# Three moved pieces at the start of a four-layer kernel: decay rates, condition columns and rotation tables

## The chip, the cores and the metric

The kernel runs on one core of a Trainium2 chip. The metric is device time in microseconds (us) of one execution, the median of three runs. The core has five engines with a queue of instructions each: PE (matmul), DVE (vector), ACT (activation), POOL (GpSimd) and SP, which here only issues DMAs. Each queue is executed in its order; an instruction whose semaphores have not come holds up everything behind it on its engine.

## The reference

The input `x` is 256 rows of 1024. Two layers of a first model are applied to it (`first_block`): an even layer, whose one projection gives query, key, value, gates and the input `u` of a diagonal state-space scan, and an odd layer (indexed attention). Then two layers of a second model (`second_block`), which is conditioned on a vector `c` and has a second stream of rows, the context.

```python
# even layer of the first block (cut)
q, k, v, gate_a, u, gate_b = split_cols(hn @ w_in, EVEN_SPLITS)
q, k = rms_norm(q, q_g), rms_norm(k, k_g)
att = swa_sink_attention(q, k, v, sinks, rel_bias) * silu(gate_a)
ssm = s5_mixer(u, log_dt, a_re, a_im, ...) * silu(gate_b)   # x_t = a * x_(t-1) + b u_t
# second block (cut)
mod   = silu(c) @ ada_w[i] + ada_b[i]                       # six rows of shifts, scales, gates
mod_c = silu(c_ctx) @ ada_w[i] + ada_b[i]
# its second layer is a chunked scan (SSD) with the decay rates
A = -exp(A_log)
```

## The kernel before

The program is written in Tile: the Python text gives every instruction with its engine and a priority (the order in which it is written), and a scheduler sets the order in which each engine's queue holds them. A change of the text near the start therefore also changes the order of work far behind it.

**Weights.** A weight tile is 128x1024 words (512 KB). SP issues its DMA into one of three `raw` buffers (L167), ACT makes a rounded high part `h` (L178), DVE the remainder `l` (L179), and PE multiplies both with the high and low part of the normalised rows (`nhx`, `nlx`), for each 128 columns or rows: high times high and low, then remainder times high. There are two buffers each of `h` and `l`.

**The start.** The rows are normalised and transposed in eight pieces; ACT writes `nhx` (L329), DVE `nlx` (L330). Then PE makes, in the text's order, `u` from weight tiles 1 to 4 (`pu`), the query from tiles 5 to 8 and key and value from 9 and 10 (`pdx`), and the gates from 11 to 18 (`pg`). Beside this DVE prepares the state-space parameters (`sv`, `fr`, `bb`, `bd`, L466 to L539), whose pieces PE transposes (`pbt`, `pct`).

**Query and key norm** (`head_norm`, `rstd`): ACT squares, DVE sums (`ss`, L405), POOL makes the mean (L285) and the power -1/2 (L286), DVE multiplies (`qn`, L407), PE transposes (`pqt` for the query, `pkt` for the key). This is done once for each half of the rows: query half 0, query half 1, key half 0, key half 1.

**The rotation tables.** The scan is turned into a real one by cosines and sines for 256 positions; POOL makes them from the small tables `tr` (L642 to L647, six instructions of 128x512 for two of the sixteen states' groups) in the tile `tabs`. The first two sets, twelve instructions, are for `q == 0`.

**The decay rates** (end of `late_params`, L372 to L379): a DMA of 64 words `A_log`, a power on POOL (L373), three small DVE steps (L374 to L376), one PE product and a copy to `A_row`. They lie in the tile `rp`, which also holds the other late parameters. `A_row` is read only in the last layer (`step_sizes`).

**The condition columns** (`cond_columns`): two small DMAs (`crows`), a tanh on ACT, a DVE step, one PE transpose (`pcc`, L864) and one DVE copy to `cT` (L866). All products `pada` of the condition with `ada_w` (L894, weights in `aw` and `araw`, 512 KB each) need `cT`. They are called from `ctx_start`, a hook of the even layer, and PE uses them to fill its time.

Of the kernel before, what the change touches and what calls it, by code (L numbers as in the profile page):

```python
# [8 lines left out]
F32 = mybir.dt.float32  # L9
# [3 lines left out]
ALU = mybir.AluOpType  # L13
# [75 lines left out]
def build(tc, A):  # L89
# [5 lines left out]
    def D(name):  # L95
        return A[name]

    def dram(a, off, ap):
        return bass.AP(tensor=a.tensor, offset=a.offset + off, ap=ap)
# [26 lines left out]
    marks = {}  # L126
# [6 lines left out]
    def after(mark):  # L133
        return tc.issue_after(marks[mark]) if mark is not None else ExitStack()
# [146 lines left out]
    def rstd(ss, n, cnt, key):  # L281
        t = wk.tile([128, 16], F32, tag="rs0" + key[:1])
        r = wk.tile([128, 16], F32, tag="rs1" + key[:1])
        with tc.high_priority(offset=WPRI):
            G.tensor_scalar(t[:, :cnt], ss, 1.0 / n, 1e-6, op0=ALU.mult, op1=ALU.add)  # L285
            G.tensor_tensor(r[:, :cnt], t[:, :cnt], nhalf[:, :cnt], op=ALU.pow)  # L286
        return r[:, :cnt]

    sums = {}
# [62 lines left out]

    def late_params():
        rp = cx.tile([128, 512], F32, tag="ntc", name="rp")
        pa_r, pb_r, a_diag = rp[:, 0:128], rp[0:96, 128:256], rp[0:64, 256:320]
        a_log, a_pos = rp[0:64, 320:321], rp[0:64, 321:323]
        V.memset(pa_r, 0.0)
        for r0, name, n in ((16, "norm_mix_g_2", 16), (32, "norm_ffn_g_2", 16),
                            (48, "ev_glu_b", 8), (56, "ev_ssm_d", 4), (60, "ssm_norm_g_2", 16),
                            (80, "ssm_conv_b_2", 32)):  # L360
            rows(pa_r, r0, name, n)
        for r, name, n in ((76, "ev_q_norm_g", 64), (77, "ev_k_norm_g", 64), (78, "od_q_norm_g", 128),
                           (79, "od_k_norm_g", 128)):
            SY.dma_start(pa_r[r:r + 1, :], dram(D(name), 0, [[0, 1], [0, 128 // n], [1, n]]))
        rows(pb_r, 0, "ssm_conv_w_2", 96)
        pp = psx.tile([128, 512], F32, tag="m")
        T.transpose(pp[:, 0:128], pa_r, ident)
        T.transpose(pp[:, 128:224], pb_r, ident[:96, :96])
        V.tensor_copy(par[:, 16:224], pp[:, 16:224])
        for lo, hi in ((60, 76), (80, 112), (128, 224)):  # L370
            V.tensor_scalar(par[:, lo:hi], pp[:, lo:hi], 0.5, None, op0=ALU.mult)
        SY.dma_start(a_log, dram(D("ssm_A_log_2"), 0, [[1, 64], [1, 1]]))  # L372
        G.tensor_tensor(a_pos[:, 0:1], ebase[0:64, 0:1], a_log, op=ALU.pow)  # L373
        V.tensor_scalar(a_log, a_log, -e_del, 1.0, op0=ALU.mult, op1=ALU.add)  # L374
        V.scalar_tensor_tensor(a_pos[:, 1:2], a_pos[:, 0:1], -1.0, a_log, op0=ALU.mult, op1=ALU.mult)
        V.tensor_scalar(a_diag, ident[0:64, 0:64], a_pos[:, 1:2], None, op0=ALU.mult)  # L376
        pp = psx.tile([128, 512], F32, tag="m", name="pp")
        mm(pp[:, 0:64], m_le[0:64, 127:128].to_broadcast([64, 128]), a_diag, True, True)
        V.tensor_copy(A_row, pp[:, 0:64])  # L379
# [41 lines left out]
    def even_layer(hook):  # L421
        with ExitStack() as st:
# [2 lines left out]
            NW = 2304  # L425
            actk = norm_T(xt, g_norm[:, 0:8], None, "x", psx)
            wx.on_pool = LP[0]

            uT = p.tile([128, 4, 256], F32, name="uT")
            QT = p.tile([128, 4, 256], F32, name="QT")  # L430
# [199 lines left out]
            for q in range(4):  # L630
                py = psx.tile([128, 512], F32, tag="m", name="py")
                for jj in range(2):
                    ct, sn = (tabs[:, jj, z_] for z_ in range(2))
                    x1 = xp1
                    i4 = slice(4 * q + 2 * jj, 4 * q + 2 * jj + 2)

                    def hi(z):
                        return z[:, i4, 16:32][:, :, :, None].to_broadcast([128, 2, 16, 16])

                    def lo(z):  # L640
                        return z[:, i4, 0:16][:, :, None, :].to_broadcast([128, 2, 16, 16])
                    G.tensor_tensor(ct, hi(cos_), lo(cos_), op=ALU.mult)  # L642
                    G.tensor_tensor(x1, hi(sin_), lo(sin_), op=ALU.mult)
                    G.tensor_tensor(ct, ct, x1, op=ALU.subtract)
                    G.tensor_tensor(sn, hi(sin_), lo(cos_), op=ALU.mult)
                    G.tensor_tensor(x1, hi(cos_), lo(sin_), op=ALU.mult)
                    G.tensor_tensor(sn, sn, x1, op=ALU.add)  # L647
                    for j in range(2 * jj, 2 * jj + 2):
                        i = 4 * q + j
                        pv = psx.tile([128, 2, 256], F32, tag="m", name="pv")  # L650
                        for ri in range(2):
                            mm(pv[:, ri], BT[32 * j:32 * j + 32, ri, q], uT[32 * j:32 * j + 32, q], True, True)
                        cb = ct[:, j % 2].rearrange("p a b -> p (a b)")[:, None, :].to_broadcast([128, 2, 256])
                        sb = sn[:, j % 2].rearrange("p a b -> p (a b)")[:, None, :].to_broadcast([128, 2, 256])
                        m1 = sl.tile([128, 2, 256], F32, tag="m1", bufs=2)
                        m2 = sl.tile([128, 2, 256], F32, tag="m2", bufs=2)
                        V.tensor_tensor(m1, pv, cb, op=ALU.mult)
                        V.tensor_tensor(m2, pv, sb, op=ALU.mult)
                        G.tensor_tensor(m1[:, 0], m1[:, 0], m2[:, 1], op=ALU.subtract)
                        G.tensor_tensor(m1[:, 1], m1[:, 1], m2[:, 0], op=ALU.add)  # L660
                        mg = mag[:, i:i + 1].to_broadcast([128, 256])
                        for ri in range(2):
                            V.tensor_tensor_scan(m1[:, ri], mg, m1[:, ri], 0.0, op0=ALU.mult, op1=ALU.add)
                        V.tensor_tensor(m2, m1, sb, op=ALU.mult)
                        for ri in range(2):
                            V.scalar_tensor_tensor(m1[:, ri], m1[:, ri], (1.0, -1.0)[ri], cb[:, ri],
                                                   op0=ALU.mult, op1=ALU.mult)
                        o = py[32 * j:32 * j + 32, 0:256]
                        cs = slice(32 * j, 32 * j + 32)
                        mm(o, CT[:, 0, q, cs], m1[:, 0], True, False)  # L670
                        mm(o, CT[:, 1, q, cs], m1[:, 1], False, False)
                        mm(o, CT[:, 0, q, cs], m2[:, 1], False, False)
                        mm(o, CT[:, 1, q, cs], m2[:, 0], False, True)
                y = uT[:, q]
                y2 = xw.tile([128, 256], F32, tag="ntx", name="y2")
                V.scalar_tensor_tensor(y, y, ssm_d[:, q:q + 1], py[:, 0:256], op0=ALU.mult, op1=ALU.add)
                S.activation(y2, y, AF.Square)
                V.tensor_scalar(y2, y2, 0.044715, 1.0, op0=ALU.mult, op1=ALU.add)
                V.tensor_tensor(y2, y2, y, op=ALU.mult)
                S.activation(y2, y2, AF.Tanh, scale=math.sqrt(2 / math.pi))  # L680
                V.scalar_tensor_tensor(y, y2, 1.0, y, op0=ALU.add, op1=ALU.mult)
                if q in (1, 2):
                    attention(2 - q)
# [172 lines left out]
    def cond_columns():  # L856
        cr2 = cx.tile([16, 256], F32, tag="adaev", name="crows")
        cr, th = cr2[:, 0:128], cr2[:, 128:256]
        rows(cr, 0, "c_2", 8)
        SY.dma_start(cr[8:16], dram(D("c_ctx_2"), 0, [[128, 8], [1, 128]]))  # L860
        S.activation(th, cr, AF.Tanh, scale=0.5)
        V.scalar_tensor_tensor(th, th, 1.0, cr, op0=ALU.add, op1=ALU.mult)
        pt = psc.tile([128, 512], F32, tag="m", name="pcc")
        T.transpose(pt[:, 0:16], th, ident[:16, :16])  # L864
        V.memset(cT, 0.0)
        V.tensor_scalar(cT[:, :, 0:2].rearrange("p k v -> p v k"), pt[:, 0:16].rearrange("p (v k) -> p v k", v=2),  # L866
                        0.5, None, op0=ALU.mult)
# [270 lines left out]
    cst_ = {}  # L1138

    def ctx_start():  # L1140
        cond_columns()
        ada_rows(0)
        for grp in range(2):
            ada_pe(0, grp)
        ada_finish(0, 0, 2)
# [360 lines left out]
    hooks = {0: [c_start], 1: [c_qkv, c_attend]}  # L1506
    sc_b = even_layer(lambda i: [f() for f in hooks[i]])
    odd_layer(sc_b)
    c_ffn()
    x_attention()  # L1510
    tc.cur_priority += 2000000
# [31 lines left out]
```

## Time and profile before

| | before |
|---|---|
| median of 3 runs | 1568.19 us (1567.0 to 1572.32) |
| profiled execution: its own time, its span | 1569.01 us, 1567.2 us |
| PE, DVE, ACT, POOL busy | 1479.1, 1110.6, 771.3, 304.2 us |
| mean granted PE clock | 0.975 |

A row of a group or a timeline gives times in us from the span's start; "idle before" is the time in which that engine did nothing just ahead, and the arrow names what ended it. The granted clock is a share of full speed.

### The profile page before, as it was taken

The page shows a single profiled execution, that of the slowest core. Times are in us where ns is not written, and L with a number is a line of the kernel's source. Part 1 is how long each engine was busy: PE and PEld are TensorE (multiplying, and loading weights), DVE is VectorE, ACT ScalarE, POOL GpSimd, SP SyncE. Part 2 cuts the span into 40 slices and gives each one's busy share as a digit, 9 for nine tenths or more (in the row PEclk, how much of TensorE's full clock was granted, in tenths as well). Part 3 has the DMA queues.
Part 4 walks back from the last instruction along what each step waited for, and adds up shares of the span by engine and source line. Part 5 has one row for each costly group of instructions (what it writes and reads, how often), then busy time and mean ns, then how long its engine had stood idle before and what let it go on. Part 6 is the DMA issues. An engine that isn't in the chain of part 4 may idle for free. (4 is left out here: it accounts for less than half of the span.)

```text
span 1567.2 us, 26910 instructions
## 1 busy us (share of the span) xinstructions
PE 1479.1 (94%) x10532; PEld 1263.1 (81%) x10532; DVE 1110.6 (71%) x1825; ACT 771.3 (49%) x1386; POOL 304.2 (19%) x247
## 2 busy tenths in 40 slices
PE   6799998999999999999989999889899999799998
PEld 5574555786898888687779999888789998699997
DVE  6779996667766778666556665478988876665665
ACT  4433446654545455576444444445455544454444
POOL 2415660000100100000000000238966400200000
PEclk9899999999999999999999999898999999999999
DMA  8784565566665767633666465454534433455664
GB/s 252 237 224 143 185 172 164 142 190 211 192 187 169 219 204 201 224 109 101 199 209 190 161 186 181 126 135 123 128 106 129 109 97 121 156 164 187 194 188 135
DMA packets 306174, 264.56 MB, mean 169 GB/s; under 512 B 27441, under 2 KB 260703, under 8 KB 306048
## 3 DMA queue, kind: packets, MB, share of 16 engines
q1 hardware_dynamic: 306048, 262.85, 56.2%
q8 instruction: 83, 1.36, 0.4%
q14 instruction: 43, 0.35, 0.1%
HBM read 261.47 MB, written 1.34 MB: 168 GB/s over the span
## 5 line engine op out<-in xcount | busy, mean ns | idle before, releaser
L179 DVE TENSOR_TENSOR l<-raw,h 128x1024 fp32r<-128x1024 f32 (+2 forms) x366 | 453.4, 1241 | 268.0 <-ACT h L178 237.6
L178 ACT ACTIVATE h<-raw 128x1024 fp32r<-128x1024 f32 (+2 forms) x374 | 389.0, 1042 | 411.2 <-PE pdx L129 103.9
L129 PE MATMUL pffnx<-nhx,h 128*128 128x256 f32 x704 | 170.4, 282 | 0.0
L129 PE MATMUL pffnx<-nlx,h 128*128 128x256 f32 x704 | 170.1, 282 | 0.2 <-DVE nlx L349 0.2
L129 PEld LDWEIGHTS pffnx<-nhx,h 128*128 128x128 f32 x704 | 134.3, 191 | 1.6 <-issue 1.6
L129 PEld LDWEIGHTS pffnx<-nlx,h 128*128 128x128 f32 x704 | 133.9, 190 | 1.5 <-issue 0.8
L307 POOL TENSOR_TENSOR sums<-sums,nhalf 128x1 f32<-128x1 f32 x20 | 13.0, 652 | 536.3 <-DVE sums L303 523.4
L129 PE MATMUL pffnx<-nhx,l 128*128 128x256 f32 x704 | 96.8, 280 | 0.0
L129 PE MATMUL pffnc<-nhc,h 128*128 128x256 f32 x352 | 88.9, 287 | 0.4 <-ACT nhc L348 0.4
L129 PEld LDWEIGHTS pffnx<-nhx,l 128*128 128x128 f32 x704 | 88.4, 189 | 0.4 <-issue 0.4
L129 PE MATMUL pffnc<-nlc,h 128*128 128x256 f32 x352 | 87.9, 285 | 0.1
L179 POOL TENSOR_TENSOR l<-raw,h 128x1024 fp32r<-128x1024 f32 (+1 forms) x8 | 18.5, 2312 | 353.8 <-PE pdx L129 200.5
L129 PE MATMUL pdx<-h,nhx 128*128 128x256 f32 (+1 forms) x256 | 84.8, 347 | 1.4 <-DVE cv L1284 1.3
L129 PE MATMUL pdx<-h,nlx 128*128 128x256 f32 (+1 forms) x256 | 83.0, 341 | 0.0
L894 PE MATMUL pada<-araw,cT 128*32 128x256 f32 x704 | 72.7, 401 | 10.7 <-DMA araw<-ada_w 9.8
L129 PE MATMUL pcvx<-nhx,h 128*128 128x256 f32 x256 | 73.8, 298 | 3.8 <-DVE cv L1284 3.8
L129 PE MATMUL pdx<-h,fh 128*128 128x256 f32 (+1 forms) x264 | 77.2, 318 | 0.0
L129 PE MATMUL pdx<-h,fl 128*128 128x256 f32 (+1 forms) x264 | 77.1, 317 | 0.0
L129 PE MATMUL pcvx<-nlx,h 128*128 128x256 f32 x256 | 71.8, 290 | 0.0
L129 PEld LDWEIGHTS pffnc<-nhc,h 128*128 128x128 f32 x352 | 66.5, 189 | 2.9 <-ACT nhc L348 1.0
L129 PEld LDWEIGHTS pffnc<-nlc,h 128*128 128x128 f32 x352 | 66.6, 189 | 2.1 <-DVE nlc L349 0.5
L129 PE MATMUL pdx<-l,nhx 128*128 128x256 f32 (+1 forms) x256 | 58.5, 344 | 1.4 <-DVE l L179 1.3
(620 smaller groups left out, 3875.9 us busy)
## 6 DMA issues: line engine op xcount, KB each, us to landing
araw<-ada_w SPq DMA_DIRECT2D x88, 512.0 KB
raw<-ffn_w_gate SPq DMA_DIRECT2D x66, 512.0 KB
raw<-ffn_w_up SPq DMA_DIRECT2D x66, 512.0 KB
raw<-ffn_w_down SPq DMA_DIRECT2D x54, 512.0 KB
raw<-ssm_w_in SPq DMA_DIRECT2D x48, 512.0 KB
raw<-od_w_in SPq DMA_DIRECT2D x25, 512.0 KB
raw<-attn_w_qkv SPq DMA_DIRECT2D x24, 512.0 KB
raw<-attn_w_o SPq DMA_DIRECT2D x32, 256.0 KB
```

The source lines that it names most:

```text
L129: i = T.matmul(out, l, r, start=start, stop=stop)
L178: S.activation(h[:, :n], raw[:, :n], AF.Copy)
L179: (G if self.on_pool > 0 else V).tensor_tensor(l[:, :n], raw[:, :n], h[:, :n].bitcast(F32), op=ALU.subtract)
L307: G.tensor_tensor(s[:, 3:4], s[:, j - 1:j], nhalf[:, 0:1], op=ALU.pow)
L894: T.matmul(pt[32 * q:32 * q + 32, 0:256], cT[:, k, :], raw[:, q * 256:(q + 1) * 256], start=k == 0, stop=k == 7, tile_position=(0, 32 * q))
```

## The change

Four edits. The decay rates become a function `decay_rates`, called behind the odd layer, with a tile `ar` of their own. `cond_columns` is called in the even layer right behind the first norm instead of in `ctx_start`. `rstd` notes its last instruction, and the twelve table instructions for `q == 0` are put under `after("rshe")`: the scheduler may place them only once the power of the first query half has been placed.

```diff
@@ rstd
-            G.tensor_tensor(r[:, :cnt], t[:, :cnt], nhalf[:, :cnt], op=ALU.pow)
+            i = G.tensor_tensor(r[:, :cnt], t[:, :cnt], nhalf[:, :cnt], op=ALU.pow)
+        marks.setdefault("rs" + key, i.ins)
@@ late_params
-        pa_r, pb_r, a_diag = rp[:, 0:128], rp[0:96, 128:256], rp[0:64, 256:320]
-        a_log, a_pos = rp[0:64, 320:321], rp[0:64, 321:323]
+        pa_r, pb_r = rp[:, 0:128], rp[0:96, 128:256]
...
+    def decay_rates():
+        ar = con.tile([64, 68], F32, name="ar")
+        a_diag, a_log, a_pos = ar[:, 0:64], ar[:, 64:65], ar[:, 65:67]
         SY.dma_start(a_log, dram(D("ssm_A_log_2"), 0, [[1, 64], [1, 1]]))
         G.tensor_tensor(a_pos[:, 0:1], ebase[0:64, 0:1], a_log, op=ALU.pow)
-        V.tensor_scalar(a_log, a_log, -e_del, 1.0, op0=ALU.mult, op1=ALU.add)
-        V.scalar_tensor_tensor(a_pos[:, 1:2], a_pos[:, 0:1], -1.0, a_log, op0=ALU.mult, op1=ALU.mult)
+        V.tensor_scalar(ar[:, 67:68], a_log, -e_del, 1.0, op0=ALU.mult, op1=ALU.add)
+        V.scalar_tensor_tensor(a_pos[:, 1:2], a_pos[:, 0:1], -1.0, ar[:, 67:68], op0=ALU.mult, op1=ALU.mult)
@@ even_layer
             actk = norm_T(xt, g_norm[:, 0:8], None, "x", psx)
             wx.on_pool = LP[0]
+            cond_columns()
...
-                    G.tensor_tensor(ct, hi(cos_), lo(cos_), op=ALU.mult)
...
+                    with after(None if q else "rshe"):
+                        G.tensor_tensor(ct, hi(cos_), lo(cos_), op=ALU.mult)
...
@@ ctx_start
-        cond_columns()
         ada_rows(0)
@@ end of build
     odd_layer(sc_b)
+    decay_rates()
     c_ffn()
```

How the queues change is seen in the built programs. First DVE, at the end of the first norm; `nlx` is the low part of the normalised rows, `rp` here the decay rates, `sv` and `turn` the state-space parameters. Before:

```order
L466 COPY sv_192<-psp_217 128x48
L470 TENSOR_TENSOR sv_192<-sv_192 128x16
L475 TENSOR_TENSOR turn_225<-sv_192 128x16
L503 TENSOR_TENSOR sv_192<-sv_192 128x16
L374 TENSOR_SCALAR rp_425<-rp_425 64x1
L476 TENSOR_SCALAR turn_225<-turn_225 128x16
L330 SCALAR_TENSOR_TENSOR nlx_132<-pntx_171,par_111,nhx_131 128x256
L375 SCALAR_TENSOR_TENSOR rp_425<-rp_425 64x1
```

The same place now (lines 330, 466 and so on have become 331, 471 and so on):

```order
L872 TENSOR_SCALAR cT_114<-pcc_185 128x2x8
L331 SCALAR_TENSOR_TENSOR nlx_132<-pntx_162,par_111,nhx_131 128x256 x2
L331 SCALAR_TENSOR_TENSOR nlx_132<-pntx_171,par_111,nhx_131 128x256
L471 COPY sv_201<-psp_226 128x48
L475 TENSOR_TENSOR sv_201<-sv_201 128x16
L480 TENSOR_TENSOR turn_234<-sv_201 128x16
L508 TENSOR_TENSOR sv_201<-sv_201 128x16
L481 TENSOR_SCALAR turn_234<-turn_234 128x16
L331 SCALAR_TENSOR_TENSOR nlx_132<-pntx_171,par_111,nhx_131 128x256
```

The step of the decay rates ahead of the last `nlx` is gone, and `cT`, which stood forty instructions behind it, is now written before the last four `nlx`.

Then POOL, at the query norm; `t` and `r` are the mean and the power of one half (128x8 for the query, 128x2 for the key), `tabs` and `x1` the rotation tables. Before, after the first thirteen table instructions:

```order
L646 TENSOR_TENSOR x1_196<-tr_193 128x512
L647 TENSOR_TENSOR tabs_929<-tabs_929,x1_196 128x512
L643 TENSOR_TENSOR x1_196<-tr_193 128x512
L285 TENSOR_SCALAR t_545<-ss_543 128x8
L286 TENSOR_TENSOR r_546<-t_545,nhalf_105 128x8
L285 TENSOR_SCALAR t_561<-ss_559 128x8
L286 TENSOR_TENSOR r_562<-t_561,nhalf_105 128x8
L285 TENSOR_SCALAR t_639<-ss_637 128x2
L286 TENSOR_TENSOR r_640<-t_639,nhalf_105 128x2
L285 TENSOR_SCALAR t_653<-ss_651 128x2
```

Now:

```order
L285 TENSOR_SCALAR t_546<-ss_544 128x8
L286 TENSOR_TENSOR r_547<-t_546,nhalf_105 128x8
L648 TENSOR_TENSOR tabs_930<-tr_202 128x512
L649 TENSOR_TENSOR x1_205<-tr_202 128x512
L651 TENSOR_TENSOR tabs_930<-tr_202 128x512
L648 TENSOR_TENSOR tabs_930<-tr_202 128x512
L651 TENSOR_TENSOR tabs_930<-tr_202 128x512
L285 TENSOR_SCALAR t_562<-ss_560 128x8
L650 TENSOR_TENSOR tabs_930<-tabs_930,x1_205 128x512
L285 TENSOR_SCALAR t_640<-ss_638 128x2
L286 TENSOR_TENSOR r_563<-t_562,nhalf_105 128x8
L652 TENSOR_TENSOR x1_205<-tr_202 128x512
```

The tables have gone from ahead of the norm into it: five stand between the two query halves, and the power of the second half (`r_563`) stands behind a sixth one and behind the mean of the first key half (`t_640`). The power of the second key half comes after six more.

Last PE, at the fifth weight tile (`pdx` from `h_470` before, `h_471` now); `aw` are six tiles of `ada_w`. Before:

```order
L129 MATMUL pdx0_466<-h_470,nlx_132 128x512
L864 MATMUL pcc_1461<-misc_79,crows_1456 128x16
L129 MATMUL pdx0_466<-l_471,nhx_131 128x512 x2
L129 MATMUL pdx1_467<-h_470,nhx_131 128x512
L129 MATMUL pdx1_467<-h_470,nlx_132 128x512
...
L129 MATMUL pdx1_467<-l_471,nhx_131 128x512 x2
L894 MATMUL pada_1468<-aw_1469,cT_114 32x256 x4
```

Now:

```order
L129 MATMUL pdx0_467<-h_471,nlx_132 128x512
L900 MATMUL pada_1460<-aw_1461,cT_114 32x256 x4
L900 MATMUL pada_1460<-aw_1467,cT_114 32x256 x3
L129 MATMUL pdx0_467<-l_472,nhx_131 128x512 x2
L900 MATMUL pada_1460<-aw_1467,cT_114 32x256
L900 MATMUL pada_1460<-aw_1473,cT_114 32x256 x4
L900 MATMUL pada_1460<-aw_1479,cT_114 32x256
L129 MATMUL pdx1_468<-h_471,nhx_131 128x512
```

The transpose `pcc` has left this place (it is now the ninth row of PE's queue), and the products with `cT` stand between those of the fifth weight tile. Further back the orders differ through the odd layer and the context's FFN, and are the same from the last layer on.

## Rows read from the trace of the kernel before

**Rows 1.** The page: PE's busy time, its share of the span, instructions.
```profile
PE 1479.1 (94%) x10532; PEld 1263.1 (81%) x10532; DVE 1110.6 (71%) x1825; ACT 771.3 (49%) x1386; POOL 304.2 (19%) x247
```

**Rows 2.** Stretches: span, busy of PE, PEld, DVE, ACT, POOL; PE clock; DMA share, GB/s.
```profile
20.00:40.00 20.00, 14.74 (x94) 13.59 (x94) 15.45 (x34) 8.06 (x10) 9.14 (x8) 0.83 0.87 308
40.00:60.00 20.00, 15.50 (x93) 9.26 (x94) 16.49 (x26) 6.84 (x11) 11.61 (x10) 0.83 0.58 200
60.00:80.00 20.00, 17.19 (x124) 12.51 (x124) 12.33 (x23) 9.21 (x14) 4.62 (x6) 0.83 0.90 269
500.00:600.00 100.00, 100.00 (x670) 87.65 (x669) 73.28 (x112) 51.31 (x79) 7.35 (x4) 1.00 0.70 212
```

**Rows 3.** Timeline, 20 to 30 us, POOL, DVE and PE: start, duration, what.
```profile
22.80 0.53 POOL L373 TENSOR_TENSOR rp<-ebase,rp 64x1 f32<-64x1 f32 x1 [8.55 <-DMA rp<-ssm_A_log]
23.37 0.15 DVE L374 TENSOR_SCALAR rp<-rp 64x1 f32<-64x1 f32 x1 [3.93 <-POOL rp L373]
24.04 0.58 PE L129 MATMUL pu<-nlx,h 128*128 128x256 f32 x1 [4.29 <-DVE nlx L330]
24.42 1.91 PE L129 MATMUL pu<-nhx,l 128*128 128x256 f32 x8
29.15 1.07 PE L129 MATMUL pu<-nhx,l 128*128 128x256 f32 x8
```

**Rows 4.** Timeline, 37 to 61 us, DVE and PE, around `cT`.
```profile
37.90 0.98 DVE L506 TENSOR_TENSOR sv<-sv 128x16 f32<-128x16 f32 x1
41.04 0.16 DVE L511 TENSOR_TENSOR sv<-sv 128x16 f32<-128x16 f32 x1
43.84 0.17 DVE L866 TENSOR_SCALAR cT<-pcc 128x16 f32<-128x16 f32 x1
44.07 4.49 PE L894 MATMUL pada<-aw,cT 128*32 128x256 f32 x40 [5.29 <-DVE cT L866]
59.99 1.07 PE L894 MATMUL pada<-aw,cT 128*32 128x256 f32 x16
```

**Rows 5.** Stretch in which POOL makes the first tables; columns as in rows 2.
```profile
33.50:45.00 11.50, 6.21 (x45) 4.59 (x47) 11.33 (x16) 3.78 (x6) 9.97 (x9) 0.88 0.90 349
```

**Rows 6.** Timeline, 28 to 39 us, SP and ACT: the sixth weight tile.
```profile
28.99 0.38 SPq L167 DMA_DIRECT2D raw<-ev_w_in  x1
38.96 1.06 ACT L178 ACTIVATE h<-raw 128x1024 fp32r<-128x1024 f32 x1 [2.66 <-DMA raw<-ev_w_in]
```

**Rows 7.** Stretch in which that tile is under way; columns as in rows 2.
```profile
35.00:40.00 5.00, 3.78 (x19) 2.62 (x18) 4.86 (x6) 1.90 (x3) 4.66 (x5) 1.00 1.03 401
```

**Rows 8.** Timeline, 49 us, PE: the first product of tile 6.
```profile
49.19 0.48 PE L129 MATMUL pdx<-h,nhx 128*128 128x512 f32 x1
```

**Rows 9.** Timeline, 55 to 80 us, POOL and PE: query and key norm.
```profile
55.76 2.12 POOL L643 TENSOR_TENSOR x<-tr 128x512 f32<-128x512 f32 x1
64.68 0.20 POOL L285 TENSOR_SCALAR t<-ss 128x8 f32<-128x8 f32 x1 [6.80 <-DVE ss L405]
64.97 1.69 POOL L286 TENSOR_TENSOR r<-t,nhalf 128x8 f32<-128x8 f32 x1
68.45 1.12 PE L560 MATMUL pqt<-misc,qn 128*128 128x128 f32 x4 [2.22 <-DVE qn L407]
74.49 0.66 PE L560 MATMUL pqt<-misc,qn 128*128 128x128 f32 x4
74.73 0.19 POOL L285 TENSOR_SCALAR t<-ss 128x2 f32<-128x2 f32 x1 [5.83 <-DVE ss L405]
79.69 0.38 PE L129 MATMUL pg<-nhx,h 128*128 128x256 f32 x1
```

**Rows 10.** A group on POOL, 19 to 65 us: count, busy us, mean ns, idle before.
```profile
L644 POOL TENSOR_TENSOR tabs<-tabs,x 128x512 f32<-128x512 f32 x2 | 2.5, 1269 | 0.0
```

**Rows 11.** Who PE waited for, whole span: us in total, times, longest.
```profile
PE pada L894 <- DMA araw<-ada_w: 9.8, 11, 1.7
```

**Rows 12.** A stretch of the scan; columns as in rows 2.
```profile
120.00:140.00 20.00, 17.51 (x100) 8.33 (x98) 19.27 (x28) 5.31 (x14) 15.38 (x14) 0.98 0.55 174
```

More of the change, by code (lines that the diff above doesn't have):

```diff
@@ L641, in lo @@
                         return z[:, i4, 0:16][:, :, None, :].to_broadcast([128, 2, 16, 16])
-                    G.tensor_tensor(ct, hi(cos_), lo(cos_), op=ALU.mult)
[L643 to L647, printed above, removed]
+                    with after(None if q else "rshe"):
+                        G.tensor_tensor(ct, hi(cos_), lo(cos_), op=ALU.mult)
+                        G.tensor_tensor(x1, hi(sin_), lo(sin_), op=ALU.mult)
+                        G.tensor_tensor(ct, ct, x1, op=ALU.subtract)
+                        G.tensor_tensor(sn, hi(sin_), lo(cos_), op=ALU.mult)
+                        G.tensor_tensor(x1, hi(cos_), lo(sin_), op=ALU.mult)
+                        G.tensor_tensor(sn, sn, x1, op=ALU.add)
                     for j in range(2 * jj, 2 * jj + 2):
```

## The prediction

> **What bounds the kernel now.** I read the page first, then busy time by stretches, then who PE waits for, then the timeline of the stretches in which it waits. PE is busy 1479.1 of 1567.2 us [rows 1]: the kernel is PE's work plus the 88 us in which PE has none. Further on PE has few gaps (500 to 600 us is full, [rows 2]), so whatever is gained earlier should be carried through as a shift. The gaps that this change can reach lie at the start: in 20 to 80 us PE is idle 5.3 + 4.5 + 2.8 us, and its granted clock is 0.83 there [rows 2], so some of its busy time runs at the lower of its two levels (1.2 instead of 2.4 GHz).
>
> Two waits make most of it. The first is at 19.75 us: PE wants the last `nlx`, which stands on DVE behind a step of the decay rates, which waits for POOL, which waits for the DMA of `A_log`. DVE loses 3.93 us, PE 4.29, and the eight products that follow take 1.91 us where the same eight take 1.07 later [rows 3]. The second is at 38.8 us: PE waits 5.29 us for `cT`, and 40 products take 4.49 us, 0.112 each, where 16 take 1.07 later, 0.067 each [rows 4]. `cT` is late because DVE, in its order, is still at the state-space parameters: while POOL makes tables DVE is busy 11.33 of 11.5 us [rows 5], and steps on 16 columns take 0.98 us instead of 0.16 [rows 4].
>
> **The change part by part.**
>
> *Decay rates.* One DMA, one POOL power (0.53 us), three DVE steps, one product and a copy leave the path and come back where DVE and PE work for the odd layer; nothing is added, and 0.5 us of DVE there is covered by its 27 us per 100 of idle time [rows 2]. The wait of 4.29 us goes. PE would be at the last `nlx` at about 20.0 us. The clock is then not lowered there: the slow pace lasts somewhat short of the row at 29.15, some 22 products, at 0.105 us each (from the 1.91 and 1.07 for eight), 2.3 us. At the first tile that is 6.6 us.
>
> *Condition columns.* Two DMA issues, a tanh, a DVE step, a transpose and a copy come into the first norm. DVE gets about 0.45 us more there, estimated from like steps of 0.15 to 0.3 us, and PE a transpose of 0.25, between pieces for which both wait anyway; I take 0, with 0.5 as the bound. SP issues two DMAs more ahead of the parameters and three fewer behind them. The 5.29 us wait for `cT` goes.
>
> These gains do not add up to 12 us and more, because a third wait stands behind them: the sixth weight tile. It lands at 38.96 us [rows 6], and the DMA engines are then full (share 1.03, [rows 7]), with six `aw` tiles ahead of it. Its issue waited for a `raw` buffer until 28.99 [rows 6]; now that buffer should be free some 5 us earlier, and SP comes to it right behind the `aw` tiles, at about 26.3. As it queues behind the same bytes I give it 1.5 us, not 2.7: landing at 37.4, high part (1.06 us) at 38.5. PE is there before, at about 34.5, and idles 4 us. So its first product comes at 38.5 instead of 49.19 [rows 8]: **10.7 us earlier**. The bounds: 9.2 if it lands as now, 11.9 if it keeps the whole 2.7.
>
> *From there to the query's sums.* Before, 49.19 to 64.6 us is 15.4 us of PE at work [rows 8, 9]. Now PE starts at the lower clock (eight products of 512 columns and four transposes, about 2.4 us more), and the parameter pieces, the context's norm and three remainders, which DVE partly had behind it, fall into the same stretch; against that, no tables run beside them. By adding up DVE's and ACT's steps in the new order, each at the time of a like step, I estimate the sums at 55.3, 16.8 us after: **1.4 us given back**, between 0 and 4.
>
> *Tables behind the query norm.* Their twelve instructions are moved, not removed. The first query half is served as before (3.8 us from its mean, at 64.68, to its transposes, at 68.45, [rows 9]): transposes at about 59.0. For the second half POOL first makes five tables, about 1.27 us each [rows 10], then a sixth, then the mean of the key's first half, whose sum comes 6.3 us after the transposes (68.45 to 74.73, [rows 9]): 65.3. The power of the second half, 1.7 us, ends at 67.2, its multiplication at 67.9. PE, which had its transposes at 74.49 without a wait, is done with the key's products at 64.8 and waits 3 us. It then runs at the lower clock again, about 0.8 us more than before to the gates. So the gates begin at 73.9 instead of 79.69: a gain of 5.8, or **3.5 us given back**; between 0, if DVE's sums come late enough, and 8, if every table takes the 2.12 us of the slowest row [rows 9]. The last key half's power waits for six more tables, until about 78 us; PE asks for it at 79.9, behind two gate tiles, so that costs nothing.
>
> A rule of the Trainium skill (SBUF — State Buffer, Who interferes with whom) speaks against this part: a DVE instruction with two SBUF inputs and a GpSimd one that reads SBUF exclude each other for the whole instruction. The small steps of 0.98 us beside POOL, 0.16 without, agree with it [rows 4, 5]. By it that time is not saved but passed on, to the remainders of the gate weights, which have two SBUF inputs, and the whole would come to 1567 us, as in the second rival below.
>
> *The rest.* Behind the scan the scheduler's order differs up to the last layer, with the same instructions. I give that 0 us, plus or minus 4, less than half of the 9.8 us that PE now waits for `ada_w` in all [rows 11]: an order made by the same scheduler should have about as many gaps.
>
> **The sum.** -10.7 + 1.4 + 3.5 = -5.8 us, against the profiled execution's 1569.01: 1563.2. That execution is 0.8 above the median of the runs shown; against the median I predict 1562.4 us. A difference under 0.3%, 4.7 us, can hardly be told from none here.
>
> **The rivals.**
>
> *More is kept.* The second wait for the query's power is covered by other work, or the sixth tile lands earlier: 10.7 less 1.4 stays, 9.3, 1559. For it: DVE's sums for the second half and for the key may come together. Against it: the power stands behind the key's mean in POOL's queue, whatever DVE does.
>
> *The tables take it back.* They run beside DVE's remainders and lengthen each other: five at 2.12 instead of 1.27 us cost 4.3 more in the second query half, and the gain is 1.5: 1567. For it: the row of 2.12 us [rows 9]. Against it: a table took 1.27 in the mean, with DVE full [rows 5, 10].
>
> *The scan hides the start.* From 100 us on DVE is the bound, 19.27 of 20 us [rows 12]. If DVE came to the scan no earlier than now, 1568. Against it: its scan steps wait for the gates' remainders, which come earlier with PE.
>
> *Slower.* PE waits for `ada_w` eleven times, 0.89 us each [rows 11], because two `araw` buffers are refilled from a queue that serves weights too, and that order has changed. Twelve more such waits outside the scan turn the gain into a loss of 4.7 us; with fourteen the time is 1575. Against it: many of the present ones lie in the scan, where DVE is the bound, and the DMA share is 0.55 there [rows 12].
>
> **How the numbers follow.** The forecast, a gain of 4 to 8 us, has 0.42 (own range 1559 to 1565); more kept 0.18; taken back 0.22; hidden 0.08; slower 0.10. Faster by over 0.3%: the first, but for a little, and the second, 0.58. Same: 0.32. Slower: 0.10. The range 1556 to 1570 leaves out the slower case and the ends of the others.
>
> **What would show it.** Right: no wait of PE for the last `nlx` or for `cT`; small `sv` steps at 0.16 us throughout; PE waiting some 4 us for the sixth tile, which lands at 36 to 39 us; first gate product at 72 to 76. On POOL the second half's power some 9 us or more behind the first's, and PE waiting about 3 us for it. From there all stages up to the last layer early by the same 5 to 7 us. Wrong: a sixth tile as late as now, a gate stage that starts later than 78, or more and longer waits for `araw` in 300 to 1000 us.

## The result, and the profile after

The changed kernel takes 1583.13 us (median of five runs, 1579.02 to 1585.74), the kernel before 1568.19 in five runs beside it: 1.0095 times as long, with an interval of 1.0076 to 1.0114. I had forecast 1562.4. All instructions are still there, and PE's engine total has grown. The page of the changed kernel, whose span is 1580.5 us (as in [rows 1], 16 us more PE time for the same 10532 instructions):

```profile
PE 1495.1 (95%) x10532; PEld 1273.7 (81%) x10532; DVE 1102.6 (70%) x1825; ACT 772.0 (49%) x1386; POOL 306.6 (19%) x247
```

The stretches that stand in [rows 2] and [rows 12], now (span, busy of PE, PEld, DVE, ACT, POOL with counts; PE clock; DMA share, GB/s):

```profile
20.00:40.00 20.00, 17.20 (x142) 13.13 (x141) 14.25 (x41) 7.40 (x9) 2.67 (x1) 1.00 0.80 288
40.00:60.00 20.00, 16.82 (x90) 10.42 (x90) 13.80 (x28) 11.97 (x18) 4.56 (x5) 0.91 0.95 327
60.00:80.00 20.00, 14.80 (x104) 13.62 (x105) 8.05 (x10) 5.26 (x8) 19.28 (x18) 0.83 0.67 220
120.00:140.00 20.00, 18.02 (x95) 9.00 (x95) 19.41 (x29) 6.63 (x13) 15.43 (x13) 1.00 0.39 120
500.00:600.00 100.00, 99.76 (x620) 83.39 (x619) 72.31 (x109) 50.70 (x74) 6.28 (x4) 1.00 0.66 204
```

The first 60 us are better: 142 products from 20 to 40 us where there were 94, at a clock of 1.00 instead of 0.83. From 60 to 80 us POOL is busy 19.28 us, mostly with the tables, and PE is idle 5.2. From 500 to 600 us PE is as full as before, but its count is 620 instead of 670, a mix of other products, since another part of the program stands there.

The timeline of the same places as in [rows 3], [rows 6], [rows 8] and [rows 9] (rows left out are marked):

```profile
20.45 0.39 PE L129 MATMUL pu<-nlx,h 128*128 128x256 f32 x1 [0.40 <-DVE nlx L331]
20.67 1.12 PE L129 MATMUL pu<-nhx,l 128*128 128x256 f32 x8
...
24.09 4.29 SPq L898 DMA_DIRECT2D aw<-ada_w  x6
28.42 0.57 SPq L898 DMA_DIRECT2D araw<-ada_w  x1
29.09 0.49 SPq L167 DMA_DIRECT2D raw<-ev_w_in  x1
...
39.41 1.06 ACT L178 ACTIVATE h<-raw 128x1024 fp32r<-128x1024 f32 x1 [7.80 <-DMA raw<-ev_w_in]
40.52 0.80 PE L129 MATMUL pdx<-h,nhx 128*128 128x512 f32 x1 [2.70 <-ACT h L178]
...
57.10 0.20 POOL L285 TENSOR_SCALAR t<-ss 128x8 f32<-128x8 f32 x1 [9.22 <-DVE ss L409]
57.39 2.73 POOL L286 TENSOR_TENSOR r<-t,nhalf 128x8 f32<-128x8 f32 x1
...
60.90 1.11 PE L565 MATMUL pqt<-misc,qn 128*128 128x128 f32 x4 [1.92 <-DVE qn L411]
...
68.17 1.65 POOL L286 TENSOR_TENSOR r<-t,nhalf 128x8 f32<-128x8 f32 x1
70.60 1.04 PE L565 MATMUL pqt<-misc,qn 128*128 128x128 f32 x4 [4.30 <-DVE qn L411]
...
76.24 0.38 PE L129 MATMUL pg<-nhx,h 128*128 128x256 f32 x1
```

Both waits are gone but for a rest: PE waits 0.40 us for the last `nlx` where it waited 4.29, the eight products behind it take 1.12 us instead of 1.91 (the granted clock is 1.00 from 20 to 40 us), and no wait for `cT` is left. The third wait, for the sixth weight tile, is where the prediction put it, and so is the fourth, 4.30 us for the second query half. The gates begin at 76.24 instead of 79.69. So the start does gain, 3.45 us, and the loss is somewhere else.

Whom PE waited for in the whole span (us in total, times, longest), first the group of [rows 11]:

```profile
PE pada L900 <- DMA araw<-ada_w: 8.4, 7, 2.1
...
PE pqt L565 <- DVE qn L411: 6.2, 2, 4.3
PE py L129 <- DVE m L672: 4.7, 5, 2.2
```

The two waits that are new, for `qn` and `m`, make under 9 us more, and others have shrunk: PE is even idle less in all than before (1580.5 - 1495.1 = 85.4 us, 88.1 before). So the time is in PE's busy part, and not by the clock, whose mean is 0.977 (0.975 before). That is what the experiments had to explain.

Two numbers are used from here on. The first is the count of PE's products in a stretch. The second is the **pace**: in the timeline of PE, the distance from the start of a single row of one 256-column product to the start of the next row, averaged over all those in the span that lie within 0.105 to 0.125 us (some 4,500 to 4,900 a run). It is 0.1162 us before and 0.1176 after the change.

### The profile page after: what moved, and what is told of

It reads as the page before. It is cut to its first block, busy times and chain, and to the rows that moved or that the text cites. A ratio compares the mean times of both kernels' runs of the same rounds, so it can differ in the third digit from the quotient of the medians.

```text
span 1580.5 us, 26895 instructions
## 1 busy us (share of the span) xinstructions
PE 1495.1 (95%) x10532; PEld 1273.7 (81%) x10532; DVE 1102.6 (70%) x1825; ACT 772.0 (49%) x1386; POOL 306.6 (19%) x247
## 5 line engine op out<-in xcount | busy, mean ns | idle before, releaser
L179 DVE TENSOR_TENSOR l<-raw,h 128x1024 fp32r<-128x1024 f32 (+2 forms) x366 | 458.4, 1253 | 273.6 <-ACT h L178 227.5
L129 PEld LDWEIGHTS pdx<-h,nhx 128*128 128x128 f32 x256 | 51.5, 201 | 11.5 <-ACT h L178 4.2
```

Of the source, the lines that this page charges most:

```text
L129: i = T.matmul(out, l, r, start=start, stop=stop)
L179: (G if self.on_pool > 0 else V).tensor_tensor(l[:, :n], raw[:, :n], h[:, :n].bitcast(F32), op=ALU.subtract)
```

## The experiments

### One part alone (e1 to e4)

e1 moves the decay rates alone, e2 the condition columns alone, e3 puts the tables alone behind the query norm, e4 moves decay rates and columns but not the tables. Each takes its hunks of the diff and leaves the others.

e1: 

> Only the decay rates are moved behind the odd layer; condition columns and tables stay where they were. Theory of the order: the change gains at the start (up to 4 us at the first tiles), the scan hands that back, and the scheduler, which lays out everything anew, puts the even and odd layers' products ahead of the context's on PE (its last product of the odd layer's index keys stands at row 1520 of the queue instead of 1586, as at 1532 in the full change); PE then runs out of filler between 220 and 560 us: 1574 to 1583 us. Rival, the local one: the loss is made by the tables behind the query norm (PE's wait of 4.3 us for the query and of 4.7 us in the scan), so this part alone is as good as or better than before: 1562 to 1568.

e2: 

> Only the condition columns are moved next to the first norm. Theory of the order: the wait for cT goes, but the order of PE behind the scan is again one with the x products early (row 1533 for the end of the index keys): 1572 to 1582 us. Local rival: no tables in the query norm, so 1560 to 1567.

e3: 

> Only the first tables are put behind the power of the first query half. Theory of the order: here PE's order goes the other way (index keys end at row 1622, later than before at 1586), so the loss is no more than the local waits make: 1566 to 1573 us. Local rival: this is the part that costs, 1574 to 1583 us, with PE waiting 4 us or more for the query's transposes and as much for the scan's products.

e4: 

> Decay rates and condition columns are moved, the tables stay. Both gains of the start without the tables' waits. Theory of the order: the gain at the gates is larger than in the full change (8 us or more), but the order on PE is the same as in the full change as far as the index keys (row 1532), so it still ends at 1572 to 1580 us. Local rival: 1557 to 1563.

| run | median us | ratio to before | pace, us |
|---|---|---|---|
| before | 1570.15 | | 0.1162 |
| e1 decay rates | 1587.25 | 1.0121 [1.0086, 1.0157] | 0.1174 |
| e2 columns | 1579.12 | 1.0057 [1.0033, 1.0081] | 0.1159 |
| e3 tables | 1574.46 | 1.0035 [1.0019, 1.0052] | 0.1157 |
| e4 decay rates, columns | 1583.30 | 1.0089 [1.0059, 1.0118] | 0.1176 |

The local rival is out: for e1, e2 and e4 it gave 1557 to 1568 and they took 1579 to 1587, the tables with their waits cost least of the parts, and the part that takes one wait away and adds none costs most. My theory of the order (the scheduler lays out both models' work anew, and the gain of the start is lost in that) held for e2 alone: e3 is 1.5 us above its range, which is the lower end of the rival's, e4 is 3.3 above, and e1 4.3. So that theory was not enough. What the two worst kernels and the full change have in common is the pace, 0.1174 to 0.1176 us, and an edit: `decay_rates` has a tile `ar` of its own in the pool `con`. The built programs list the tiles' addresses. `ar` takes 288 bytes in each partition, and so the tiles of the pools allocated behind it on that side of SBUF move by 288 bytes, among them the normalised rows `nhx` (from 21152 to 21440) and `nlx`. The weight tiles, allocated from the other side, stay (`h` at 184288). In e2 and e3 the rows lie as before.

### The place of the tiles (e5 to e9, e12 to e14)

e5 and e9 are the kernel before with a tile that nobody writes or reads; all engines' queues are those of before, word for word.

```diff
     odd_layer(sc_b)
+    con.tile([64, 68], F32, name="pad")      # e5; [64, 24] in e9
```

e6, e7, e8 and e12 only make `ar` wider (e8 and e12 in the kernel of e4):

```diff
-        ar = con.tile([64, 68], F32, name="ar")
+        ar = con.tile([64, 80], F32, name="ar")   # e6, e8; 128 in e7, 88 in e12
```

e13 (in the full change) and e14 (in the kernel before) move the weights, and the tiles allocated behind them on that side, instead:

```diff
+    es.enter_context(pool("pr", right=True)).tile([64, 24], F32, name="padr")   # e13; 16 in e14
     wx = Weights("x", *WX, SY, es)
```

e5: 

> The kernel before with one more thing: a tile of 64x68 words in the pool con, never written or read, at the place where the decay rates' tile ar is allocated. All instructions and their order on all engines are those of before; only the addresses of the tiles behind it in the on-chip memory move by 288 bytes (the normalised rows from 21152 to 21440, so from 32 to 0 beyond a multiple of 64), while the weight tiles stay. Theory of the place: products follow each other 1 to 2% more slowly because their operands lie elsewhere (0.1176 us from one 256-column product to the next instead of 0.1162), and that alone makes 1580 to 1588 us, with all waits as before. Rival, the theory of the order: nothing in the order has changed, so 1567 to 1572 us.

e6: 

> The full change, with ar 80 instead of 68 words wide, so that the tiles behind it move by 320 bytes and lie 32 beyond a multiple of 64 as before. The order of all engines is that of the full change. Theory of the place: the products' pace is 0.116 us again and the time falls by some 15 us, to 1563 to 1570. Theory of the order: as the full change, 1579 to 1586 us.

e7: 

> The full change, with ar 128 words wide: the tiles behind it move by 512 bytes, which keeps their place relative to multiples of 64, 128, 256 and 512. Theory of the place: 1563 to 1570 us, as with 320 bytes if it is the multiple of 64 that matters; if it is a larger multiple, this one is fast and the one with 320 is not. Theory of the order: 1579 to 1586 us.

e8: 

> Decay rates and condition columns moved, tables left as before, with ar 80 words wide. Theory of the place: the index keys end 4 us earlier than before, as in the same kernel with 68 words, and nothing takes that back in pace: 1560 to 1569 us. Theory of the order: 1578 to 1587 us.

e9: 

> The kernel before with an unused tile of 64x24 words at the place of the decay rates' tile: nothing else, the order of all engines as before. The tiles behind it move by 96 bytes, so the normalised rows go from 32 to 0 beyond a multiple of 128. So far 32 gave 0.1160 us from product to product, 64 gave 0.1175 and 96 gave 0.1194. Theory of the place within 128 bytes, rising with it: 0 gives 0.115 or less and the time falls under 1567, to 1550 to 1566 us. Rival: what counts is whether the rows lie at the same place in 64 bytes as the weights, or a place within 256 or 512 bytes; then 0 is no better than the others, 1567 to 1590 us.

e12: 

> Decay rates and condition columns moved, tables left, ar 88 words wide: the tiles behind it move by 352 bytes, the normalised rows lie at a multiple of 128. Same order as with 512 bytes. Theory of the place, rising within 128 bytes: the quickest of the three with this order, 5 to 15 us under the one with 512 bytes and under the kernel before: 1553 to 1566 us. Rival (no advantage of a multiple of 128): 1566 to 1590 us.

e13: 

> The full change with ar 68 words wide, as given, and an unused tile of 64x24 words ahead of the weights' buffers on the other side of the memory, so that the weight tiles move by 96 bytes, from 96 to 0 beyond a multiple of 128, while the rows stay at 64. The order on all engines is that of the full change. Theory of the distance: rows and weights are half of 128 apart again, the pace is 0.116 us and the time that of the full change with 512 bytes, 1573 to 1579 us. Rival, the place of the rows alone: pace 0.1175, 1580 to 1586 us.

e14: 

> The kernel before, with an unused tile of 64x16 words ahead of the weights' buffers: only the weight tiles and what lies behind them move, by 64 bytes, from 96 to 32 beyond a multiple of 128, which is where the rows lie. The order on all engines is that of before. Theory of the distance: rows and weights at one place, as in the run with 320 bytes, pace 0.119 us, and 1580 to 1592 us. Rival, the place of the rows alone: pace 0.116, 1566 to 1571 us.

The table gives where the rows `nhx` and the weights `h` begin beyond a multiple of 128 bytes, by address, and how far apart the two are on that circle. The kernel before took 1569.68 us beside e5 to e8, 1567.27 beside e9 and e12, and 1568.66 beside e13 and e14.

| kernel | rows, weights | apart | median us | ratio to before | pace, us |
|---|---|---|---|---|---|
| before | 32, 96 | 64 | 1568.19 | | 0.1162 |
| e7 change, `ar` 512 bytes | 32, 96 | 64 | 1575.93 | 1.0032 [1.0017, 1.0047] | 0.1159 |
| e13 change, weights moved | 64, 0 | 64 | 1574.66 | 1.0040 [1.0022, 1.0058] | 0.1168 |
| change | 64, 96 | 32 | 1583.13 | 1.0095 [1.0076, 1.0114] | 0.1176 |
| e5 before, unused tile | 64, 96 | 32 | 1582.89 | 1.0081 [1.0060, 1.0103] | 0.1174 |
| e9 before, unused tile | 0, 96 | 32 | 1577.21 | 1.0064 [1.0041, 1.0087] | 0.1173 |
| e12 as e4, `ar` 352 bytes | 0, 96 | 32 | 1578.84 | 1.0077 [1.0058, 1.0096] | 0.1171 |
| e6 change, `ar` 320 bytes | 96, 96 | 0 | 1588.84 | 1.0114 [1.0096, 1.0131] | 0.1194 |
| e8 as e4, `ar` 320 bytes | 96, 96 | 0 | 1588.13 | 1.0103 [1.0080, 1.0126] | 0.1195 |
| e14 before, weights moved | 32, 32 | 0 | 1584.53 | 1.0101 [1.0061, 1.0140] | 0.1195 |

e5 decides the first question: an unused tile, with no instruction and no order changed, makes the kernel before 13 us slower. Its page:

```profile
PE 1494.3 (94%) x10532; PEld 1272.6 (80%) x10532; DVE 1108.5 (70%) x1825; ACT 771.1 (49%) x1386; POOL 302.5 (19%) x247
```

Beside [rows 1], PE has grown by 15.2 us, and DVE, ACT and POOL have not: whatever the place does, it does to PE. The full change with 512 bytes, which keeps every place, has PE back at nearly its old total:

```profile
PE 1481.7 (94%) x10532; PEld 1261.9 (80%) x10532; DVE 1100.7 (70%) x1825; ACT 772.0 (49%) x1386; POOL 304.9 (19%) x247
```

That is 7 us better than the change as given (10 by the ratios, which go by the kernel before beside each run), and still 6 more than the theory of the place allowed (1563 to 1570): something else costs too, which the next group looks for. My expectations for e6 and e8 were wrong: I had thought of multiples of 64, and 320 bytes made it worse. With e9 and e12 a pace that rises with the rows' place fell too, since 0 is no better than 64. What fits is the distance between rows and weights, and e14 put that to the test: it moves the weights only, onto the place of the rows, and gets the pace of e6 in the order of before. The rival (the place of the rows alone) gave 1566 to 1571 for it. A stretch of the last FFN, in which PE is never idle, at a clock of 1.00, and makes only products of 256 columns (columns as above), first before, then the change, then e14, then e13:

```profile
1400.00:1430.00 30.00, 30.00 (x267) 30.00 (x266) 19.76 (x29) 14.86 (x22) 0.00 (x0) 1.00 0.66 195
```

```profile
1400.00:1430.00 30.00, 30.00 (x255) 30.00 (x255) 18.63 (x26) 14.42 (x22) 0.00 (x0) 1.00 0.64 188
```

```profile
1400.00:1430.00 30.00, 30.00 (x252) 30.00 (x252) 18.69 (x28) 13.93 (x21) 0.00 (x0) 1.00 0.62 182
```

```profile
1400.00:1430.00 30.00, 30.00 (x267) 30.00 (x266) 19.25 (x27) 14.88 (x23) 0.00 (x0) 1.00 0.67 194
```

The reader sees no wait in any of the four, and 267, 255, 252 and 267 products in the same 30 us. One stretch is not the whole: e13 has the full number here and the time of e7, but a pace of 0.1168 over its span, between the two levels. So for products of 256 columns the worst case is settled: the same place. That rows at 64 are as good as at 32 once the weights are half of 128 away is shown for the time of e13, and only half for its pace. Products of 512 columns, in which a weight tile moves and the rows are the weights at rest, rank the cases otherwise: in the same traces (pairs within 0.215 to 0.250 us) they follow each other in 0.2312 us before, 0.2332 with the change and 0.2299 in e14, so there the same place is not the worst. Which accesses meet in there, no run shows.

### The order alone (e10, e11, e15)

With the place kept, what do the edits do? e10 is e4 and e11 is e1 with `ar` 128 words wide. e15 moves a DMA whose 64 words the start does not need:

```diff
-    SY.dma_start(dtb_row, dram(D("ssm_dt_bias_2"), 0, [[0, 128], [1, 64]]))
...
     odd_layer(sc_b)
+    SY.dma_start(dtb_row, dram(D("ssm_dt_bias_2"), 0, [[0, 128], [1, 64]]))
```

e10: 

> Decay rates and condition columns moved, tables left as they were, with ar 128 words wide, so that all places are those of before within 512 bytes. What the two edits do by their order alone: the pace is 0.116 us as before. Theory of order and place together: of the 13 us that the same edits cost with 68 words, the place made 7 to 13, so 1566 to 1575 us. Rival: the gain of 10 us at the first gate product is kept once the place is right: 1557 to 1563 us.

e11: 

> The decay rates alone moved, with ar 128 words wide, places as before within 512 bytes. Theory of order and place together: the 17 us that this edit cost with 68 words fall to what the order makes, 1569 to 1578 us, and the pace is 0.116 us. Rival: the decay rates' move costs by its order or by its work behind the odd layer, and the place was nothing here: 1583 to 1590 us.

e15: 

> The kernel before with one small DMA moved: the 64 words of dtb_row, which only the second model reads, are loaded behind the odd layer instead of at the start. No tile moves in memory, no work is added. The scheduler's order is another all the same: on PE the index keys end at row 1488 of the queue instead of 1586, and the last product of the context's FFN stands at 4258 instead of 4113. Theory of the order: laying the two streams out anew costs by itself, 1572 to 1580 us at a pace of 0.116 us. Rival: the parts of the change cost by what they do and the order by itself is about nothing, 1565 to 1570 us.

The kernel before took 1567.27 us beside e10 and e11, and 1567.62 beside e15.

| run, places as before | median us | ratio to before | pace, us |
|---|---|---|---|
| e10 decay rates, columns | 1569.10 | 1.0011 [0.9999, 1.0024] | 0.1160 |
| e11 decay rates | 1573.63 | 1.0041 [1.0023, 1.0059] | 0.1163 |
| e7 all parts | 1575.93 | 1.0032 [1.0017, 1.0047] | 0.1159 |
| e15 a small DMA | 1574.38 | 1.0039 [1.0024, 1.0054] | 0.1164 |

e10 less e4 is the place once more, some 12 us by ratio (1.0089 to 1.0011). e15 comes out where the theory of the order put it: a DMA of 64 words, moved, costs 0.4%. With e2 and e3 that makes six orders other than that of before, at equal places: five are slower by 0.3 to 0.6%, and one is the same. None is faster, although the gates begin earlier in all six, by 2.4 us (e15) to 9.0 (e10). Not all of this is the order, though. In the profiled executions of e11 and e15 the last FFN's products (`pffnx`) take 156.8 us from the first start to the last (1379.4 to 1536.2 in e15) instead of 153.9 (1374.4 to 1528.3 before, the same in e7 and e10), and there all queues and these places are those of before. So 2.9 us of e15's 7.9 in these executions, and of e11's 6.2, come from something that no run here separates.

How the gain is lost shows in the count of products. The stretches 0 to 100 us and 100 to 340 us, before:

```profile
0.00:100.00 100.00, 76.35 (x505) 60.40 (x506) 66.12 (x129) 42.85 (x60) 30.52 (x34) 0.90 0.81 240
100.00:340.00 240.00, 227.86 (x1409) 148.68 (x1408) 193.46 (x323) 117.49 (x289) 79.85 (x67) 0.99 0.57 169
```

and with the change:

```profile
0.00:100.00 100.00, 77.93 (x534) 62.33 (x535) 59.47 (x130) 43.60 (x61) 32.72 (x34) 0.95 0.86 257
100.00:340.00 240.00, 224.17 (x1317) 143.35 (x1316) 189.91 (x314) 112.68 (x280) 77.59 (x67) 0.96 0.51 152
```

At 100 us PE is 29 products ahead, but DVE, the bound of the scan, is just one instruction ahead (130 to 129). At 340 us PE is 63 behind (29 less 92). Three things make this up, by an estimate. PE is idle 3.7 us more in that stretch, which is 31 products at 0.1176 us. It is at the lower level of its clock for 17.1 us instead of 6.8, and there a product follows the last in 0.214 us (62.0 to 63.5 us in the change): 39 products fewer. And the slower pace costs 16 of 1317. Together that is 86 of the 92. e7, with the same order and the pace of before, has 536 and 1307 in the two stretches, so it is not the place that loses them. All six other orders at the places of before show the same: 15 to 48 products ahead at 100 us (520 in e15, 553 in e10), and 60 to 133 fewer made from 100 to 340 us (1349 in e15, 1276 in e2). The `py` products, the last step of the scan on PE (first and last start), before and with the change:

```profile
L129 PE MATMUL py<-m,CT x128: 378/379/634, 104.8 to 251.1; 128*32 128x256 f32 x128
```

```profile
L129 PE MATMUL py<-m,CT x128: 379/379/636, 96.1 to 251.3; 128*32 128x256 f32 x128
```

They begin 8.7 us earlier and end at the same time. In e10 and e15:

```profile
L129 PE MATMUL py<-m,CT x128: 379/379/636, 89.7 to 247.0; 128*32 128x256 f32 x128
```

```profile
L129 PE MATMUL py<-m,CT x128: 376/379/636, 96.8 to 237.7; 128*32 128x256 f32 x128
```

e10 is 15.1 us earlier at the first and 4.1 at the last. e15 is 8.0 earlier at the first and even 13.4 at the last, and still slower in all: a scan that ends early does not make the kernel faster. Why, e10 shows best. Its products of the odd layer's index keys (`pki`) end 6.1 us earlier than before (341.4 and 347.5), but those lie at row 1532 of PE's queue instead of 1586, so PE has 54 products fewer behind it, some 6.3 us at 0.116. The lead of the first model's rows is work that the context has not had, as I read it, and it comes back behind 750 us: the last `pada` is at 828.6 instead of 817.0. In e3, where the two models' streams are shifted the other way, the hole is in the open instead; from 780 to 840 us before,

```profile
780.00:840.00 60.00, 55.30 (x471) 48.82 (x471) 36.42 (x65) 26.58 (x48) 2.60 (x4) 0.94 0.65 196
```

and in e3:

```profile
780.00:840.00 60.00, 47.45 (x358) 41.40 (x355) 32.94 (x56) 22.67 (x40) 1.10 (x2) 0.89 0.66 178
```

There the context is done early (its FFN's last product at 722.9 instead of 737.6 us) and the rows late, and PE is idle 12.55 us instead of 4.7.

## Why the prediction was wrong, point by point

The time was outside the range, on the side to which I gave 0.10.

*The two waits go: right.* PE waits 0.40 us for the last `nlx` and not at all for `cT`, and the eight slow products at 20 us, at the lower level of the clock, are gone.

*The sixth weight tile: right wait, size off.* I let SP issue it at 26.3 and land at 37.4, first product 38.5. SP issues it at 29.09, no earlier than before (28.99), because the issues ahead of it, six `aw` tiles and one `araw`, hold SP from 24.09 to 28.99. `h` begins at 39.41 and the first product at 40.52: 8.67 us of gain, not 10.7 and just under the bound of 9.2.

*To the query's sums: right.* 16.8 us were forecast, 16.58 measured (40.52 to 57.10).

*Tables behind the query norm: right.* PE waits 4.30 us for the second half (3 forecast), whose power ends at 69.82 (67.2), and the stretch from the mean to the gates grows by 4.1 us (19.14 instead of 15.01; 3.5 forecast). Behind it DVE and POOL lengthen each other (timeline of the change, 72 to 82 us, POOL and DVE):

```profile
72.83 1.05 POOL L649 TENSOR_TENSOR x<-tr 128x512 f32<-128x512 f32 x1
...
74.48 3.85 DVE L179 TENSOR_TENSOR l<-raw,h 128x1024 fp32r<-128x1024 f32 x2 [2.25 <-ACT h L178]
75.32 1.93 POOL L652 TENSOR_TENSOR x<-tr 128x512 f32<-128x512 f32 x1
...
79.53 1.23 DVE L179 TENSOR_TENSOR l<-raw,h 128x1024 fp32r<-128x1024 f32 x1 [1.00 <-ACT h L178]
79.56 2.12 POOL L649 TENSOR_TENSOR x<-tr 128x512 f32<-128x512 f32 x1
```

Beside tables, two remainders take 3.85 us instead of twice 1.23; where the remainder comes first, at 79.53, it is the table that takes 2.12 instead of 1.05.

This agrees with the rule of the Trainium skill (SBUF — State Buffer, Who interferes with whom) that I had weighed.

*"Whatever is gained earlier should be carried through as a shift": wrong.* I read that from PE's full stretches further on. Two things are wrong in it. The scan between 100 and 250 us has DVE busy 19.41 of 20 us (120 to 140), and the rival that the scan hides the start, which I gave 0.08 because its steps "wait for the gates' remainders", took the gain whole in the change. And a full PE is no proof of a shift, since much of what fills it belongs to the other model and can only be done once.

*"The rest", 0 plus or minus 4: wrong.* "An order made by the same scheduler should have about as many gaps" does not hold of this kernel. At equal places the other orders cost 2 to 9 us, with the gain of the start in them, and e15's small DMA, moved, goes with 7, of which up to 3 may not be the order. It was not the mechanism of my slower rival: the waits for `araw` fell from 9.8 to 8.4 us (10.3 in e7).

*The place: not in the sum at all, and with "the rest" the step that failed most.* I costed `ar` at nothing, as one tile more. By the runs beside e7 it makes 7 us of the 15 (1583.13 less 1575.93), by the ratios 10 (1.0095 and 1.0032), and in the kernel before, by itself, 13. So of the 20.7 us between the forecast and the result some 2.3 are the sixth tile and what follows at the start (3.45 gained instead of 5.8), 7 to 10 the place, and 8 to 11, what is left, the time from the gates on: the lost lead and the new order. The parts do not simply add: a slower place costs 13 us in the order of before and 7 to 10 in that of the change; why it is less there, no run shows.

## What to carry to other kernels

Where a change allocates a tile, look at the addresses of the tiles behind it, and hold them while you measure: an unused tile of the same size, or the new tile rounded up to 512 bytes, tells place from work in one run. Time several executions and compare more than one stretch: the last FFN shows that the pace can differ at equal places and order too. Where a scheduler lays out two streams in one queue, a gain at the start is worth only what the next bound lets through, and an edit without any work of its own belongs beside it, to show what a new order costs by itself. When no wait has grown and the engine's busy time has, count its instructions in a stretch without waits.

## What was not expected of the hardware

PE's pace depends on where its operands lie in SBUF (the on-chip memory). With the rows and the weights 64 bytes apart, counted in a circle of 128, one 256-column product follows another in 0.1157 to 0.1168 us; with 32 bytes in 0.1171 to 0.1176; at the same place in 0.1194 to 0.1195. Products of 512 columns do not follow this ranking (0.2312, 0.2332 and 0.2299 us). The profile shows none of this as a wait: PE counts as busy and its clock as 1.00. The differences, up to 3%, are a mean; within one kernel the pace also changes from stretch to stretch. In e15, where the places and, in this stretch, the queues are those of before, 1400 to 1430 us has 257 products, not 267 (258 in e11):

```profile
1400.00:1430.00 30.00, 30.00 (x257) 30.00 (x256) 18.62 (x28) 14.88 (x22) 0.00 (x0) 1.00 0.63 182
```

What else sets it there is open, and so is whether the distance alone counts or the rows' own place too (e13).
